# Two gated pairs worked off in other places on VectorE, one turn a product later, and the last products in one piece

## The chip, the cores and the metric

The kernel runs on one core of one Trainium2 chip. A core has TensorE (PE in the profile's rows, with PEld for its weight loads), VectorE (DVE), ScalarE (ACT), GpSimd (POOL), SyncE (SP, which here only issues DMAs) and 16 DMA engines. Each engine works off its own list of instructions in order; semaphores make one wait for another. The metric is the device time of one execution in microseconds (us), less is better.

## The reference, cut to what matters

One transformer layer on 512 tokens of width 1024, all in float32: half a feed-forward block, a token mixer of two kinds of attention, a second half feed-forward block, a last normalisation.

```python
D_MODEL, SEQ, HEAD_DIM = 1024, 512, 64
D_FF = 256 * ((8 * D_MODEL // 3 + 255) // 256)          # 2816 = 22 tiles of 128

def swiglu(x, w_gate, w_up, w_down):
    return (jax.nn.silu(x @ w_gate) * (x @ w_up)) @ w_down

def reference(x, ...):
    x = x + 0.5 * swiglu(rmsnorm(x, ffn1_norm), ffn1_w_gate, ffn1_w_up, ffn1_w_down)
    x = x + token_mixer(rmsnorm(x, mix_norm), w_in, w_out, ..., rel_bias)
    x = x + 0.5 * swiglu(rmsnorm(x, ffn2_norm), ffn2_w_gate, ffn2_w_up, ffn2_w_down)
    return rmsnorm(x, final_norm)
```

The token mixer projects `h @ w_in` into queries, keys and values, runs a differential attention with 4 heads and a dilated one with 8 heads, and multiplies by `w_out`.

## The kernel before

**Precision.** A float32 operand is split into a high part h (a cast on ScalarE to the matmul's type fp32r) and a low part l (VectorE takes h from the original). A product of two such operands is three matmuls: h·h, h·l, l·h (function `mm3`, lines 169 to 171; every matmul row of the trace bears one of these lines). So each weight tile costs a cast on ScalarE (line 458, rows `w<-...`) and a subtraction on VectorE (line 462, rows `w<-...,w`).

**The feed-forward blocks.** `ffn` is called twice: "a" is the first block, "b" the second. Of the 22 tiles of 128 hidden columns the first block's gate and up products are made plainly for the first tiles; from tile n1 = 6 on, two neighbouring tiles make a pair, and a pair's gate product (and then its up product) is a product of 2 x 2 blocks, made by seven block products in place of eight, with sums of blocks before and after (Winograd's form). The seven stages, in order, are a11, s3, s2, a12, s1, a22, s4; each is 12 matmuls with 256 moving columns. They add up in four PSUM banks w, x, y, z (rows `pwga`, `pxga`, `pyga`, `pzga` for a gate, `pwua` and so on for an up product). Between the stages ScalarE copies a bank into another one (w into x after a11, x into y after s2, line 544), and VectorE and ScalarE take results out: a helper tile `rbc_n` gets z, then y plus z (after s1) and x plus z (after a22), both on line 547; ScalarE takes the silu (line 692). The next stage on the same bank waits until it has been read. Units follow each other as g6, g8, u8, g10, u10, ... (g6: the gate product of the pair of tiles 6 and 7; its up products were made plainly).

**A pair's chain.** The gated pair (g0, g1) is not used as it is: the down product is also made with seven products, so `kept` (from line 742 on) makes seven operand tiles of it. On ScalarE these are four casts (h0, h1, h3, h5), on VectorE four low parts (line 742: h0's half, h2, h4, h6) and four sums on halves of 256 columns (`t0_left`, `t0_right` on line 553, `t1_both` on line 556), 12 instructions in all. Names carry the pair: `h2a4` belongs to the pair of tiles 4 and 5. That pair is the last of the plainly made tiles; its gated tiles lie in x[6] and x[7], which are free until x is loaded anew for the residual. The gated tiles of all later pairs lie in two buffers called "ptb".

**What sets the order.** In the first block's pairs, TensorE, VectorE and ScalarE run in the order in which the code issues (`manual_schedule`). `pipeline` puts every step on a heap of events with a time and a rank (`at(time, rank, f)`, `put` for rank 0) and pops them by time; the unit is STEP, the planned length of one stage. `kept(j, t1, t0, t2)` gives each step of a chain such a time:

```python
n = max(t1, t2)
put(n, t0_left)
put(n + STEP, b2_rest)
...
late = 2 * STEP * (j > n1)
at(n + 3 * STEP + late, 1, t0_rest)
at(n + 4 * STEP + late, 1, t1_rest)
```

For the pair of tiles 4 and 5 it is called with `kept(plain, 1.5 * STEP, -STEP, 1.5 * STEP)`, where 0 is the start of the first pair's products. So a number in this code moves instructions on the queues of VectorE and ScalarE. SyncE's and GpSimd's DMAs are issued in the same order of events; a load of weights into a `raw` tile waits until VectorE has read the tile's former content.

**The seam.** Between the first block and the mixer (`seam`) the residual rows are normalised in four groups of 128 tokens and turned by TensorE (`turn`, 8 transposes a group, line 1373) into `xt` banks, from which ScalarE and VectorE make the high and low parts of the left half (groups 0 and 1) and of the right half (groups 2 and 3, `split(1, ...)`). In between run 16 steps of the first query and key products, each 12 matmuls: steps 0 to 7 use the left half alone, from step 8 on the right half is read. The turn of group 2 stands ahead of step 2, that of group 3 ahead of step 4.

**The end.** The last products of the second block (stage s4 of the second group of pairs) are made token tile by token tile. For the very last token tile, bank `banks[1]` gets the last pair's products in two halves of 256 columns; after each half ScalarE squares it and sums it up (`square`, line 1962), and after the second one `factor` makes the scale of the last normalisation (lines 1967 to 1976) and `right_out` scales and writes out (lines 1997 to 1999).

Of the kernel before, what the change touches and what calls it, by code (L numbers as in the profile page):

```python
# [18 lines left out]
ALU = mybir.AluOpType  # L19
# [89 lines left out]
def tile_macaron(ctx: ExitStack, tc, xs, xT, wf, wgu1, wst1, wdg1, wqk, wvw, wv, wo, wgu2, wst2,  # L109
# [140 lines left out]
    def ffn(wgu, wst, wdg, n0, n1, norm, early, res, nm, hooks, first=None,  # L250
# [92 lines left out]
            up_w[j] = get_w(wst[j - n1][1], f"su{nm}{j}")  # L343

        ups, up_w, g = {}, {}, {}
        left, right = slice(0, HS), slice(HS, S)


# [261 lines left out]
        def block_product(t):  # L610
            u, o, p = ops[t]
            ps = groups[u[1]]
            if t == begin[u]:
                tags = (("s", "s", "mm", "mm"), ("mm",) * 4)[u[1]] + ("t",) * 2
                made[u] = [pp.tile([P, S], F32, tag=tag, name=f"pt{u[1]}{n}",
                                   bufs=4 if tag == "mm" else 2)[:] for n, tag in enumerate(tags)]
            b = made[u]
            pw, pz, pv = b[:2], b[2:4], b[4:]
            banks = {"w": pw, "z": pz, "v": pv}[o[1]]
            n = len(ps)  # L620
            if final is not None and (u[1], o[0]) == (1, "s4"):
                if p == n - 1:
                    for tt in range(2):
                        for q in range(n):
                            h, l = made[t - n + 1 + q]
                            if tt == 1 and q == n - 1:
                                bh, bl = hs[ps[q]][o[2]]
                                for c in (left, right):
                                    mm3(banks[1][:, c], bh[:, P:], bl[:, P:], h[:, c], l[:, c], False, True, True)
                                    final(f"half {c.start}", starts[t + 1], put, banks)  # L630
                                continue
                            block_mms(banks, o, ps[q], q, n, h, l, (tt,))
                            if q == 0 or q == n - 1:
                                final(f"s4 {tt} {int(q > 0)}", starts[t + 1] - n * STEP // 2 * (1 - tt),
                                      put, banks)
                return
            h, l = made.pop(t)
            block_mms(banks, o, ps[p], p, n, h, l, (0, 1))
            if p == n - 1:
                block_step(starts[t + 1], u, o[0], pw, pz, pv, banks)  # L640
# [91 lines left out]
        def kept(j, t1, t0, t2):  # L732
# [79 lines left out]
            put(t0 + STEP, b11)  # L812
            put(t0 + 2 * STEP, b11_rest)
            put(t1 + STEP, b2)
            n = max(t1, t2)
            put(n, t0_left)
            put(n + STEP, b2_rest)
            put(n + STEP, t0_right)
# [1 line left out]
            put(n + 2 * STEP, t1_both)  # L820

            at(n + 3 * STEP, 5, t1_parts)
            late = 2 * STEP * (j > n1)
            at(n + 3 * STEP + late, 1, t0_rest)
            at(n + 4 * STEP + late, 1, t1_rest)

        def pipeline():
# [37 lines left out]
            if close is not None:  # L865
                for i in range(KD):
                    at((10 + 5 * i) * STEP, 2.9, nc.sync.dma_start, x[i],
                       xn[i % 4 * P:(i % 4 + 1) * P, i // 4 * S:(i // 4 + 1) * S])
                close(at, starts[begin["t", 1]], starts[-1], ah, al)
                kept(plain, 1.5 * STEP, -STEP, 1.5 * STEP)  # L870
            if n1 + 1 not in up_w:
                up_weights(n1 + 1)
            for i in range(2):
# [455 lines left out]
    def seam(step):  # L1329
# [75 lines left out]
                if n == 5:  # L1405
                    split(0, now[0])
        for c in range(16):
            if c in (2, 4):
                pe(0.8, turn, 1 + c // 2)
            if c == 4:  # L1410
                split(1, now[0])
            pe(1.36, step, c)
        for _, _, f, a in sorted(todo, key=lambda e: (e[0], e[1])):
# [545 lines left out]

    def square(n, tt, y, scale=1.0):  # L1960
        junk = tp.tile([P, S], F32, tag="ptb", name=f"junk{n}{tt}")
        A.activation(junk[:, :y.shape[-1]], y, AF.Square, scale=scale, accum_out=number(n, tt))

    def factor(t0, n):

# [38 lines left out]
    def final(what, t, put, banks):  # L2004
# [9 lines left out]
        elif what == "s1":  # L2014
            for i, tt in enumerate((2, 3)):
                put(t, lambda i=i, tt=tt: V.scalar_tensor_tensor(banks[i], x[tt], 2.0, banks[i],
                                                                 op0=ALU.mult, op1=ALU.add))
                put(t + STEP, square, 0, tt, x[4 + tt])
                put(t + 2 * STEP, first_sum, tt)
                put(t + 3 * STEP, weighted, tt, 1)  # L2020
                put(t + 4 * STEP, weighted, i, 0)
        elif what == "a22":
            for tt in (0, 1):
                put(t, square, 1, tt, x[4 + tt])
            put(t, factor, 0, 2)
            for tt in (0, 1):
                put(t, left_out, tt)
        elif what.startswith("half"):
            c = int(what[5:])
            square(1 if c else 8, 3, banks[1][:, c:c + HS], 0.5)  # L2030
            if c == 0:
                V.scalar_tensor_tensor(number(2, 3), number(8, 3), 1.0 / D, number(2, 3), op0=ALU.mult, op1=ALU.add)
            else:
                factor(3, 1)
                right_out(3, banks[1])
        elif what.startswith("s4") and what.endswith("1"):
            i = int(what[3])
            square(1, 2 + i, banks[i], 0.5)
            factor(2 + i, 1)
            right_out(2 + i, banks[i])  # L2040
# [170 lines left out]
```

## Time and profile before

| | |
|---|---|
| time, median of 3 runs | 921.85 us (921.41 to 922.94) |
| the profiled execution | 922.98 us, of which span from first to last instruction 921.2 us |
| TensorE matmuls busy | 909.7 us (99%), 5793 instructions |
| TensorE weight loads busy | 819.9 us (89%) |
| VectorE busy | 721.3 us (78%), 1500 instructions |
| ScalarE busy | 554.0 us (60%), 1169 instructions |
| GpSimd busy | 95.1 us (10%) |
| moved by DMA | 142.31 MB, mean 154 GB/s |

TensorE's row is full in all 40 slices but the last, at the full granted clock. So the time is TensorE's work plus the places where it stands still. A row of the timeline reads: start, duration, engine, line, operation, output<-inputs, shape, and in brackets how long the engine had been idle and who released it. Buffer numbers are left out of the names there.

### The profile page before, as it was taken

How to read it: one execution, taken by the hardware profiler on the slowest of the kernel's cores; microseconds unless marked ns; L12 is line 12 of the kernel's file. 1: busy time of each engine (PE TensorE's matmuls, PEld its weight loads, DVE VectorE, ACT ScalarE, POOL GpSimd, SP SyncE). 2: the span in 40 equal slices, each digit the busy share in tenths (PEclk: the TensorE clock that was granted, in tenths of full speed). 3: DMA queues.
4: the chain of work that ended last, by engine and by line, in shares of the span. 5: the costliest groups of instructions: out<-in, count | busy, mean ns of one | idle time of the engine just before them, and what ended most of it. 6: DMA issues, size and time to landing. Idle time of an engine off the chain costs nothing.

```text
span 921.2 us, 16005 instructions
## 1 busy us (share of the span) xinstructions
PE 909.7 (99%) x5793; PEld 819.9 (89%) x5793; DVE 721.3 (78%) x1500; ACT 554.0 (60%) x1169; POOL 95.1 (10%) x119
## 2 busy tenths in 40 slices
PE   9999999999999999999999999999999999999996
PEld 7888998999998889888989778989999889999885
DVE  7797888888888865857865545897887778888886
ACT  7455665466668455656776676656665546665563
POOL 0001102111212000000000000011121012211100
PEclk9999999999999999999999999999999999999999
DMA  7456667787877332334433214365797279778722
GB/s 257 125 146 157 182 198 205 185 203 198 211 199 214 114 113 76 93 107 113 125 115 115 69 26 135 93 168 164 180 239 200 92 182 246 199 178 208 191 69 91
DMA packets 66239, 142.31 MB, mean 154 GB/s; under 512 B 7600, under 2 KB 8112, under 8 KB 66160
## 3 DMA queue, kind: packets, MB, share of 16 engines
q1 hardware_dynamic: 50880, 113.29, 38.2%
q0 software_dynamic: 15280, 28.01, 18.3%
q8 instruction: 45, 0.74, 0.3%
q14 instruction: 34, 0.28, 0.1%
HBM read 135.98 MB, written 2.14 MB: 150 GB/s over the span
## 4 chain that ended last, share of the span: by engine, by line
PE 88%; DVE 6%; ACT 3%; DMA 2%; issue 1%; SPq 0%; DVEq 0%; ACTq 0%
PE pt L171 5%; PE pt L169 5%; PE pt L170 5%; PE pwo L169 2%; PE pwo L171 2%; PE pwo L170 2%; PE pq L169 2%; PE pua L170 2%; PE pua L171 2%; PE pua L169 2%; PE pq L171 2%; PE pk L169 2%; PE pq L170 2%; PE pk L171 2%; PE pk L170 1%; DVE w L462 1%
## 5 line engine op out<-in xcount | busy, mean ns | idle before, releaser
L1696 ACT ACTIVATE pr<-pr,mx 128x128 f32<-128x128 f32 (+3 forms) x64 | 36.0, 563 | 36.7 <-DVE mx L1693 36.5
L1693 DVE CUSTOM_DVE_ANT_0 pr<-sc,strip 128x128 f32<-128x128 f32 (+3 forms) x64 | 30.5, 489 | 23.1 <-PE sc L1691 22.6
L394 POOL DMA_DIRECT2D s1bg<-wst_dram x10 | 8.7, 866 | 346.2 <-DVE fin L1326 234.9
L556 DVE SCALAR_TENSOR_TENSOR x<-pt,x 128x512 f32<-128x512 f32 x50 | 32.7, 687 | 14.8 <-PE pt L171 12.4
L462 DVE TENSOR_TENSOR w<-s2b,w 128x512 fp32r<-128x512 f32 x38 | 26.1, 687 | 6.8 <-ACT w L458 6.8
L458 ACT CAST w<-s2b 128x512 fp32r<-128x512 f32 x38 | 23.5, 619 | 6.7 <-DVE s2b L426 6.3
L458 ACT CAST w<-raa 128x512 fp32r<-128x512 f32 x27 | 16.4, 621 | 16.2 <-DVE raa L421 5.9
L169 PE MATMUL pwo<-w,mh 128*128 128x512 f32 x64 | 25.9, 405 | 0.0
L462 DVE TENSOR_TENSOR w<-s2a,w 128x512 fp32r<-128x512 f32 x30 | 20.6, 687 | 5.8 <-ACT w L458 5.8
L170 PE MATMUL pwo<-w,mh 128*128 128x512 f32 x64 | 25.0, 391 | 0.0
L171 PE MATMUL pwo<-w,ml 128*128 128x512 f32 x64 | 25.0, 391 | 0.0
L458 ACT CAST w<-s2a 128x512 fp32r<-128x512 f32 x30 | 18.6, 620 | 7.9 <-DVE s2a L426 7.8
L171 PE MATMUL pwgb<-xh,w 128*128 128x256 f32 x80 | 22.7, 284 | 0.2 <-DVE w L462 0.2
L169 PE MATMUL pwgb<-xh,w 128*128 128x256 f32 x80 | 22.6, 282 | 0.1
L1484 DVE TENSOR_TENSOR w<-raw_qk,w 128x512 fp32r<-128x512 f32 x24 | 16.4, 687 | 7.9 <-ACT w L1480 7.8
L170 PE MATMUL pwgb<-xl,w 128*128 128x256 f32 x80 | 22.5, 281 | 0.0
L170 PE MATMUL pxgb<-ttb,w 128*128 128x256 f32 x80 | 22.5, 281 | 0.0
L1690 PE MATMUL sc<-k,q 128*128 128x128 f32 (+3 forms) x64 | 20.5, 322 | 0.0
L1691 PE MATMUL sc<-l,q 128*128 128x128 f32 (+3 forms) x64 | 20.2, 322 | 0.0
L170 PE MATMUL pwub<-xl,w 128*128 128x256 f32 x72 | 20.2, 281 | 0.0
L171 PE MATMUL pwub<-xh,w 128*128 128x256 f32 x72 | 20.2, 281 | 0.0
L169 PE MATMUL pwub<-xh,w 128*128 128x256 f32 x72 | 20.2, 281 | 0.0
(753 smaller groups left out, 3872.5 us busy)
## 6 DMA issues: line engine op xcount, KB each, us to landing
raw_qk<-wqk_dram SPq DMA_DIRECT2D x12, 512.0 KB, 3.5
raw0bg<-wst_dram SPq DMA_DIRECT2D x10, 512.0 KB, 5.7
raw0bu<-wst_dram SPq DMA_DIRECT2D x9, 512.0 KB, 6.1
raw_gua<-wgu_dram SPq DMA_DIRECT2D x8, 512.0 KB, 3.5
raw0ag<-wst_dram SPq DMA_DIRECT2D x8, 512.0 KB, 5.5
strip<-bias_rows SPq DMA_DIRECT2D x16, 256.0 KB, 3.5
raw_wo<-wo_dram SPq DMA_DIRECT2D x8, 512.0 KB, 3.5
raw0au<-wst_dram SPq DMA_DIRECT2D x7, 512.0 KB, 6.5
```

Of the source, the lines that this page charges most:

```text
L169: T.matmul(po, wh, mh, start=first, stop=False, skip_group_check=on)
L170: T.matmul(po, wh, ml, start=False, stop=False, skip_group_check=on)
L171: T.matmul(po, wl, mh, start=False, stop=last, skip_group_check=on)
L394: nc.gpsimd.dma_start(t[:], b, accum_op=ALU.add)
L458: A.copy(made[t][0], source(t))
L462: V.tensor_tensor(l, source(t), h.bitcast(F32), op=ALU.subtract)
L556: V.scalar_tensor_tensor(o, a, f, b, op0=ALU.mult, op1=op1)
L1484: V.tensor_tensor(l[:, c:c + 512], raw[:, c:c + 512], h[:, c:c + 512].bitcast(F32), op=ALU.subtract)
L1690: T.matmul(ps[:, :w], qs[:, qi], ks[:, :w], start=True, stop=False)
L1691: T.matmul(ps[:, :w], qs[:, qi], ls[:, :w], start=False, stop=True)
L1693: V.tensor_tensor_reduce(out=pi, in0=ps[:, :w], in1=st["b"][m][:, w - 1::-1], op0=ALU.add, op1=ALU.min, scale=1.0, scalar=3.0e38, accum_ou ...
L1696: A.activation(pi, pi, AF.Exp, scale=-1.0, bias=st["mx"][:, m, i:i + 1], accum_out=st["ls"][:, m, i:i + 1])
```

## The change

Three places change.

1. The gated tiles of the first pair (6 and 7) lie in x[4] and x[5] in place of two "ptb" buffers. From `t0_left` on, this pair's chain is planned a STEP later, and its last two low parts (h4, h6) a further 4 STEP. The chain of the pair 4 and 5 starts 2.3 STEP earlier, its first part 2 STEP earlier.
2. In the seam, the turn of group 3 and the work behind it stand ahead of step 5 in place of step 4.
3. The last products of the last token tile are made with all 512 columns, and squared in one piece. The code of the halves goes, and `square` writes whole tiles.

```diff
         ups, up_w, g = {}, {}, {}
+        if close is not None:
+            g[n1] = {0: x[4], 1: x[5]}
...
-                            if tt == 1 and q == n - 1:
-                                bh, bl = hs[ps[q]][o[2]]
-                                for c in (left, right):
-                                    mm3(banks[1][:, c], bh[:, P:], bl[:, P:], h[:, c], l[:, c], False, True, True)
-                                    final(f"half {c.start}", starts[t + 1], put, banks)
-                                continue
                             block_mms(banks, o, ps[q], q, n, h, l, (tt,))
...
-            n = max(t1, t2)
+            free = close is not None and j == n1
+            n = max(t1, t2) + STEP * free
             put(n, t0_left)
...
-            late = 2 * STEP * (j > n1)
+            late = 4 * STEP if free else 2 * STEP * (j > n1)
             at(n + 3 * STEP + late, 1, t0_rest)
             at(n + 4 * STEP + late, 1, t1_rest)
...
-                kept(plain, 1.5 * STEP, -STEP, 1.5 * STEP)
+                kept(plain, -0.8 * STEP, -3 * STEP, -0.8 * STEP)
...
         for c in range(16):
-            if c in (2, 4):
+            if c in (2, 5):
                 pe(0.8, turn, 1 + c // 2)
-            if c == 4:
+            if c == 5:
                 split(1, now[0])
...
-        A.activation(junk[:, :y.shape[-1]], y, AF.Square, scale=scale, accum_out=number(n, tt))
+        A.activation(junk[:], y, AF.Square, scale=scale, accum_out=number(n, tt))
...
-        elif what.startswith("half"):
-            c = int(what[5:])
-            square(1 if c else 8, 3, banks[1][:, c:c + HS], 0.5)
-            if c == 0:
-                V.scalar_tensor_tensor(number(2, 3), number(8, 3), 1.0 / D, number(2, 3), op0=ALU.mult, op1=ALU.add)
-            else:
-                factor(3, 1)
-                right_out(3, banks[1])
```

What this moves shows in three places of the queues. In all of them x6 and x7 hold the gated tiles of the pair 4 and 5, g0a6 and g1a6 (now x4 and x5) those of the first pair, `raw...`, `s1...`, `s2...`, `s3...` are weight tiles and their sums, and the line numbers of the changed kernel are 2 to 4 off.

VectorE in the first pair's gate product, the twelve instructions that end with the sum that frees bank y for stage s4 (`rbc_n1<-pyga0`). Before:

```order
L553 TENSOR_TENSOR x6_102<-x6_102 128x256
L462 TENSOR_TENSOR w_105<-raw1ag_731,w_105 128x512
L742 TENSOR_TENSOR h2a4_870<-x7_103,h1a4_868 128x512
L553 TENSOR_TENSOR x6_102<-x7_103,x6_102 128x256
L462 TENSOR_TENSOR w_105<-s2a2_779,w_105 128x512
L556 SCALAR_TENSOR_TENSOR x7_103<-x7_103,x6_102 128x256
L556 SCALAR_TENSOR_TENSOR x7_103<-x7_103 128x256
L426 TENSOR_TENSOR s2a9_894<-s1ag_8_723,raw0ag_813 128x512
L462 TENSOR_TENSOR w_105<-raw0ag_813,w_105 128x512
L742 TENSOR_TENSOR h4a4_910<-x6_102,h3a4_888 128x512
L550 TENSOR_TENSOR g0a6_892<-pua6_716,g0a6_892 128x256
L547 TENSOR_TENSOR rbc_n1_401<-pyga0_821,rbc_n1_401 128x256
```

VectorE at the same place after the change (h2a4 and the sum on x6 stand just ahead of the first row):

```order
L430 TENSOR_TENSOR s2a2_779<-raw0ag_729,s2a2_779 128x512
L464 TENSOR_TENSOR w_105<-s1ag_6_628,w_105 128x512
L558 SCALAR_TENSOR_TENSOR x7_103<-x7_103,x6_102 128x256
L558 SCALAR_TENSOR_TENSOR x7_103<-x7_103 128x256
L464 TENSOR_TENSOR w_105<-raw1ag_731,w_105 128x512
L738 TENSOR_TENSOR h4a4_877<-x6_102,h3a4_858 128x512
L464 TENSOR_TENSOR w_105<-s2a2_779,w_105 128x512
L738 TENSOR_TENSOR h6a4_896<-x7_103,h5a4_879 128x512
L428 TENSOR_TENSOR s2a9_899<-s1ag_8_723,raw0ag_815 128x512
L464 TENSOR_TENSOR w_105<-raw0ag_815,w_105 128x512
L552 TENSOR_TENSOR x4_100<-pua6_716,x4_100 128x256
L549 TENSOR_TENSOR rbc_n1_401<-pyga0_823,rbc_n1_401 128x256
```

The chain of the pair 4 and 5 has moved ahead by two to five places, so that all of it, h6a4 too, is done before the sum; the sum of weights `s2a2` (line 428, now 430) and `w<-s1ag`, which stood just ahead of the first block, have moved behind h2a4.

ScalarE in the second pair's gate product (g8), from the copy after a11 to the silu of its first half. Before:

```order
L544 COPY pxga7_967<-pwga7_966 128x256
L458 CAST w_105<-raw1ag_815 128x512
L544 COPY rbc_n1_401<-pzga7_969 128x256
L458 CAST w_105<-s2a9_894 128x512
L780 CAST h3a6_1023<-g0a6_892 128x512
L544 COPY pyga7_968<-pxga7_967 128x256
L458 CAST w_105<-raw0au_960 128x512
L458 CAST w_105<-s3au_8_810 128x512
L790 CAST h5a6_1061<-g1a6_933 128x512
L692 ACTIVATE g0a8_1066<-pwga7_966 128x256
```

ScalarE at the same place after the change:

```order
L546 COPY pxga7_965<-pwga7_964 128x256
L460 CAST w_105<-raw1ag_817 128x512
L546 COPY rbc_n1_401<-pzga7_967 128x256
L460 CAST w_105<-s2a9_899 128x512
L546 COPY pyga7_966<-pxga7_965 128x256
L460 CAST w_105<-raw0au_958 128x512
L776 CAST h3a6_1037<-x4_100 128x512
L460 CAST w_105<-s3au_8_812 128x512
L688 ACTIVATE g0a8_1058<-pwga7_964 128x256
L460 CAST w_105<-s2a16_1041 128x512
```

The cast of h3a6 no longer stands ahead of the copy into bank y, and h5a6 no longer ahead of the silu.

VectorE in g8, the rows that end with the sum that frees bank y for g8's stage s4. Before:

```order
L428 TENSOR_TENSOR s2a9_894<-raw0ag_813,s2a9_894 128x512
L462 TENSOR_TENSOR w_105<-s1ag_8_723,w_105 128x512
L742 TENSOR_TENSOR h2a6_1002<-g1a6_933,h1a6_983 128x512
L553 TENSOR_TENSOR g0a6_892<-g1a6_933,g0a6_892 128x256
L462 TENSOR_TENSOR w_105<-raw1ag_815,w_105 128x512
L556 SCALAR_TENSOR_TENSOR g1a6_933<-g1a6_933,g0a6_892 128x256
L556 SCALAR_TENSOR_TENSOR g1a6_933<-g1a6_933 128x256
L462 TENSOR_TENSOR w_105<-s2a9_894,w_105 128x512
L742 TENSOR_TENSOR h4a6_1043<-g0a6_892,h3a6_1023 128x512
L426 TENSOR_TENSOR s2a16_1045<-s1au_8_807,raw0au_960 128x512
L462 TENSOR_TENSOR w_105<-raw0au_960,w_105 128x512
L547 TENSOR_TENSOR rbc_n1_401<-pyga7_968,rbc_n1_401 128x256
```

VectorE at the same place after the change:

```order
L430 TENSOR_TENSOR s2a9_899<-raw0ag_815,s2a9_899 128x512
L464 TENSOR_TENSOR w_105<-s1ag_8_723,w_105 128x512
L555 TENSOR_TENSOR x4_100<-x4_100 128x256
L464 TENSOR_TENSOR w_105<-raw1ag_817,w_105 128x512
L738 TENSOR_TENSOR h2a6_1018<-x5_101,h1a6_981 128x512
L555 TENSOR_TENSOR x4_100<-x5_101,x4_100 128x256
L464 TENSOR_TENSOR w_105<-s2a9_899,w_105 128x512
L558 SCALAR_TENSOR_TENSOR x5_101<-x5_101,x4_100 128x256
L558 SCALAR_TENSOR_TENSOR x5_101<-x5_101 128x256
L428 TENSOR_TENSOR s2a16_1041<-s1au_8_809,raw0au_958 128x512
L464 TENSOR_TENSOR w_105<-raw0au_958,w_105 128x512
L549 TENSOR_TENSOR rbc_n1_401<-pyga7_966,rbc_n1_401 128x256
```

The low part h4a6 has left this stretch (it comes seven rows later, in the up product), the half sum `t0_left` has come in from ahead of it, and h2a6 stands behind `w<-raw1ag`. The order of DMAs on SyncE and GpSimd is the same in both kernels.

## The prediction

> **What bounds the kernel now.** I read four views in this order: the page's busy times, the list of what TensorE waited for, TensorE's timeline at the places that list names, and there the timelines of VectorE and ScalarE.
>
> ```profile
> PE 909.7 (99%) x5793; PEld 819.9 (89%) x5793; DVE 721.3 (78%) x1500; ACT 554.0 (60%) x1169; POOL 95.1 (10%) x119
> PE pt L169 <- ACT junk L1962: 1.0, 1, 1.0
> ...
> PE pyga L169 <- DVE rbc_n L547: 0.8, 1, 0.8
> PE xt L1373 <- ACT y L1363: 0.4, 1, 0.4
> ```
>
> TensorE is full, so only its own work or its stops can give time. Each part of the change lies at one of these stops: `pyga` in the first two pairs, `xt` in the seam, `pt` at the end. The list leaves out shorter gaps; the starts of the products show them all:
>
> ```profile
> 83.38 0.28 PE L169 MATMUL pwga<-xh,w 128*128 128x256 f32 x1
> ...
> 91.78 0.28 PE L171 MATMUL pxga<-tta,w 128*128 128x256 f32 x1
> 92.82 0.39 PE L169 MATMUL pyga<-xh,w 128*128 128x256 f32 x1 [0.76 <-DVE rbc_n L547]
> ...
> 94.34 0.28 PE L169 MATMUL pwga<-xh,w 128*128 128x256 f32 x1
> ...
> 97.42 0.39 PE L169 MATMUL pxga<-txa,w 128*128 128x256 f32 x1
> ...
> 100.76 0.39 PE L169 MATMUL pyga<-txa,w 128*128 128x256 f32 x1 [0.24 <-ACT pyga L544]
> ...
> 103.98 0.38 PE L169 MATMUL pyga<-xh,w 128*128 128x256 f32 x1
> ...
> 105.50 0.28 PE L169 MATMUL pwua<-xh,w 128*128 128x256 f32 x1
> ...
> 115.44 0.28 PE L169 MATMUL pwga<-xh,w 128*128 128x256 f32 x1
> ```
>
> The rows at 83.38, 94.34, 105.50 and 115.44 begin g6, g8, u8 and g10, 84 products of the same shape each. u8 takes 115.44 - 105.50 = 9.94 us (1.42 a stage, 0.12 a product); g6 takes 10.96 and g8 11.16. Against u8's pace 1.02 + 1.22 = 2.24 us are lost at the four 0.38 to 0.39 rows, which are the first product behind each stop.
>
> **Part 1, the two chains.** It adds and removes no instruction; it moves some. Who is late at each stop:
>
> ```profile
> 82.66 0.62 ACT L458 CAST w<-s1ag 128x512 fp32r<-128x512 f32 x1 [3.10 <-PE pua L170]
> 94.33 0.64 ACT L692 ACTIVATE g1a<-rbc_n 128x512 f32<-128x512 f32 x1 [2.73 <-DVE rbc_n L547]
> 96.47 0.62 ACT L770 CAST h1a<-g1a 128x512 fp32r<-128x512 f32 x1
> 96.99 0.37 ACT L544 COPY pxga<-pwga 128x256 f32<-128x256 f32 x1
> 99.82 0.62 ACT L780 CAST h3a<-g0a 128x512 fp32r<-128x512 f32 x1 [0.92 <-DVE g0a L553]
> 100.34 0.36 ACT L544 COPY pyga<-pxga 128x256 f32<-128x256 f32 x1
> ```
> ```profile
> 83.31 0.69 DVE L462 TENSOR_TENSOR w<-s1ag,w 128x512 fp32r<-128x512 f32 x1 [2.00 <-ACT w L458]
> 85.92 0.69 DVE L462 TENSOR_TENSOR w<-raw1ag,w 128x512 fp32r<-128x512 f32 x1 [1.57 <-ACT w L458]
> 87.86 0.69 DVE L742 TENSOR_TENSOR h2a<-x,h1a 128x512 fp32r<-128x512 f32 x1 [1.25 <-ACT h1a L770]
> ...
> 91.41 0.69 DVE L742 TENSOR_TENSOR h4a<-x,h3a 128x512 fp32r<-128x512 f32 x1
> 92.01 0.42 DVE L550 TENSOR_TENSOR g0a<-pua,g0a 128x256 f32<-128x256 f32 x1
> 92.35 0.41 DVE L547 TENSOR_TENSOR rbc_n<-pyga,rbc_n 128x256 f32<-128x256 f32 x1
> ```
>
> First stop (0.92 of the 1.02: 92.82 less 91.90, one step of 0.12 behind 91.78). Stage s4 waits until VectorE has read bank y, which it does at 92.35 behind a backlog, although it idled 2.00 + 1.57 + 1.25 us shortly before. The change fills that idle time. In the new order VectorE waits at h2a4 for h1a4, which ScalarE now casts right behind `w<-s1ag`: 82.66 + 0.52 (the step from 96.47 to 96.99) + 0.62 = 83.8. From there to the sum `rbc_n<-pyga` stand, by the new order, nine instructions of 512 columns at 0.60 (91.41 to 92.01), two of 256 at 0.34 (92.01 to 92.35) and two of line 556, at most 0.60 each: at most 7.3 us, so the sum begins by 91.1 and ends 0.41 later at 91.5, ahead of 91.90. The stop goes.
>
> With it g8 begins at 93.32 (83.38 + 9.94) and its stages are due at 1.42 each. Second stop (97.42, s2 of g8 waits for the copy at 96.99, which stands behind five ScalarE instructions that begin with the silu at 94.33): that silu came late because VectorE's sum `rbc_n<-pxga` did. After the change the sum follows the end of stage a22 (about 92.1), the silu begins at 92.5, 1.8 us earlier, and the copy, 2.66 behind it as now, at about 95.2; s2 is due at 96.16. Third stop (100.76): the copy at 100.34 stood behind h3a, which waited 0.92 for VectorE; h3a6 now stands behind it, so the copy follows the end of s2 at about 97.8, and s1 is due at 99.00. Fourth stop (103.98, s4 of g8 behind VectorE's second sum): VectorE is busy without a break from the end of that silu, 93.2, on. By the new order nine instructions of 512, four of 256 and two of line 556 lie ahead of the sum: 5.40 + 1.36 + at most 1.20 = 7.96, so it ends by 93.2 + 7.96 + 0.41 = 101.6; s4 is due at 101.84. That is the thinnest cover of the four, 0.2 us or a little more. h4a6 and h6a6 (1.2 us) go into u8's time, and there VectorE waits for TensorE anyway:
>
> ```profile
> 111.38 0.42 DVE L550 TENSOR_TENSOR g0a<-pwua,g0a 128x256 f32<-128x256 f32 x1 [1.23 <-PE pwua L171]
> ```
>
> What is moved past what: the weight sum `s2a2` (line 428) falls behind h2a4, to 83.86 + 0.60 + 0.34 = 84.8, and the `raw` tile it reads is free at 85.5, where the load that takes its place is now issued at 81.38, 4.1 us earlier. SyncE's load `raw1ag`, two sums' loads and `raw0au` queue behind it:
>
> ```profile
> 81.38 0.33 SPq L402 DMA_DIRECT2D raw1ag<-wst_dram  x1
> ...
> 86.64 0.33 SPq L402 DMA_DIRECT2D raw0au<-wst_dram  x1
> raw0au<-wst_dram SPq DMA_DIRECT2D x1, 512.0 KB, 9.2
> ```
>
> The last row is the slowest landing of such a load in the next stretch. `raw0au` waits for `w<-raw1ag` on VectorE, which begins after two more instructions of 512 and two of line 556, at 87.2, and ends at 87.9 instead of 86.6; with 9.2 us it lands at 97.1. Its first reader is ScalarE's cast behind the copy that follows s2, at about 98.1. So I cost the delay at nothing, with a cover of 1.0 us; beyond it a late load stops TensorE one for one. GpSimd's accumulating DMAs for g10 follow SyncE's by the same 4 us, with all of u8 between them and their use. x[4] and x[5] are loaded anew 30 and 35 planned stages in, the chain is through after about 17: nothing.
>
> Value of part 1: between 1.02 (only the first stop goes) and 2.24 (all four). I take 2.24, since each due time is met even with the upper counts.
>
> **Part 2, the turn.**
>
> ```profile
> 350.80 0.28 PE L171 MATMUL pk<-xh,wx 128*128 128x256 f32 x1
> 351.46 1.09 PE L1373 MATMUL xt<-ident,y 128*128 128x128 f32 x8 [0.39 <-ACT y L1363]
> 350.69 0.72 ACT L1363 ACTIVATE y<-x,fin 128x512 f32<-128x512 f32 x1 [0.68 <-DVE fin L1327]
> 356.76 0.87 DVE L1315 SCALAR_TENSOR_TENSOR xl<-xt,x,xh 128x256 fp32r<-128x256 f32 x2
> ```
>
> The turn could have begun at 350.92 and began at 351.46, when `y` (350.69 + 0.72) was there: 0.54 lost. One step of 12 products, 1.43 us, put in front covers it whole. What gets late next is the right half: its parts are done at 356.76 + 0.87 = 357.6 now and about 1 us later after the change, while step 8, which reads the first two of eight, begins at 350.92 + 1.43 + 1.09 + 3 x 1.43 = 357.7 and step 11, which reads the last two, 4.3 us later. Gain 0.54; bounds 0 and 0.54.
>
> **Part 3, the end.**
>
> ```profile
> 912.62 0.28 PE L169 MATMUL pt<-kxb,h1b 128*128 128x256 f32 x1
> 914.16 0.39 PE L169 MATMUL pt<-kxb,h1b 128*128 128x256 f32 x1 [1.03 <-ACT junk L1962]
> 911.25 0.58 ACT L1962 ACTIVATE junk<-pt 128x512 f32<-128x512 f32 x1
> 911.73 0.19 ACT L1962 ACTIVATION_READ_ACCUMULATOR junk<-pt 128x1 f32 x1
> 913.65 0.36 ACT L1962 ACTIVATE junk<-pt 128x256 f32<-128x256 f32 x1
> 915.38 0.16 DVE L1967 SCALAR_TENSOR_TENSOR fin<-fin 128x1 f32<-128x1 f32 x1 [1.08 <-ACT junk L1962]
> 916.00:917.00 1.00, 0.00 (x0) 0.00 (x0) 0.82 (x5) 0.54 (x1) 0.00 (x0) 1.00 0.04 12
> ```
>
> The second half waits for the square of the first, 1.03 us, and the closing chain begins at 915.38. Whole, the last three products start 0.23 apart (a 512-column product's step, half of it 0.12) at 912.62 and end by 913.5; the square begins at 913.65 as the first half's did, since ScalarE is not free sooner, and its sum is read out 911.73 + 0.19 - 911.25 = 0.67 later. The chain begins at 914.35, 1.03 earlier, and is the same from there. The outputs ahead of it have drained by 916, as the last row shows (12 GB/s), so the last ones run into none of them. Gain 1.03; bounds -0.22 (the longer square alone, 0.58 less 0.36) and 1.03.
>
> The Trainium skill's Perfetto Trace Analysis, in Optimizing Scalar/DVE Operations, speaks against this part: where Scalar or Vector cause bubbles on other engines, breaking up instructions may let work finish sooner. By it merging would cost the 0.22 just given. The trace disagrees here, since the 1.03 wait shows that the halves did not overlap; PSUM — Partial Sum Buffer, PSUM bank collisions, has the reason: disjoint columns of one bank still collide, so the halves must take turns.
>
> **Sum.** 2.24 + 0.54 + 1.03 = 3.81 us. The profiled execution took 922.98 us (span 921.2); it would take 919.2 (span 917.4). It stood 1.1 above the median of the runs, 921.85, from which I predict 918.0.
>
> **Rivals.**
> - g8 stays tied: the thin cover of the fourth stop, or another ScalarE queueing, keeps g8's 1.22. Gain 2.59, 919.3. For it: VectorE has no break in g8. Against: the counts above are upper ones. Chance 0.13.
> - The gain of part 1 is given back: VectorE, not TensorE, sets the pace of the pairs, and TensorE stops later by what it won. Left 1.57, 920.3, within 0.2%. For it: VectorE idles little in the g stages. Against: at 111.38 it waits for TensorE in u8. Chance 0.08.
> - The whole square delays the end by 0.22 and nothing is won back: -0.22 in place of 1.03, sum 2.56, 919.3. Against: the 1.03 wait. Chance 0.02. This is how the Trainium skill's rule on breaking up (Perfetto Trace Analysis) would have it.
> - Slower: `raw0au` lands late. VectorE's wait at h2a4 delays the loads, and each us beyond the cover of 1.0 stops TensorE. It loses against before by more than 0.2% (1.84 us, about what runs of this kernel can tell) from a landing 1.0 + 3.8 + 1.8 = 6.6 us beyond the 9.2 taken; at 7 us beyond it gives 921.85 - 3.81 + 6.0 = 924.0. Against: no load of the stretch took that. With other unforeseen stops of this size, chance 0.05.
>
> **How the numbers follow.** My forecast, all stops gone, has 0.72 and gives 918.0, within 917.2 to 918.8 by the spread of the runs. Faster by over 0.2% (below 920.0) hold the forecast, the first and the third rival: 0.87. Same: 0.08. Slower: 0.05. The range reaches from 917.2 to 920.2, which takes in g8's case and half of the one that gives back.
>
> **What would show it.** Right: g6 and g8 take 9.9 us each, no `pyga` wait; the `xt` turn without idle time ahead; one 512-column square of `pt` at the end and no wait for `junk`. VectorE's stop ahead of h2a4 should last from about 81 to 83.8. Wrong: a first product of 0.39 us anywhere in g6 to g10, `raw0au` behind a ScalarE cast in the list of waits, or a gap ahead of step 8.

## The result, and the profile after

The changed kernel takes 918.58 us (median of 6 runs, 918.12 to 919.25) where the kernel before takes 922.39 (6 runs, 921.41 to 924.32): a ratio of 0.9958, 95% interval 0.9945 to 0.9971, or 3.8 us less. In a second comparison it was 919.34 against 921.97, ratio 0.9965 (0.9952 to 0.9977), or 2.6 us less. Both intervals lie below 0.998: it is faster by more than 0.2%. The profiled execution took 918.52 us, span 916.7.

The page of the changed kernel: span, busy times and the chain of work that ended last. In the kernel before the chain was 88% TensorE, 6% VectorE, 3% ScalarE and 2% DMA.

```profile
span 916.7 us, 15998 instructions
...
PE 908.7 (99%) x5790; PEld 819.8 (89%) x5790; DVE 721.2 (79%) x1499; ACT 553.7 (60%) x1167; POOL 95.2 (10%) x119
...
PE 96%; DVE 2%; ACT 1%; issue 0%; DMA 0%; DVEq 0%; SPq 0%; ACTq 0%
```

What TensorE waited for in the changed kernel (us in total, times, longest). `pyga`, `xt` and the `pt` of the end are gone from the list; the `pt` left here is a transposition in the attention and was there before.

```profile
PE warm L1139 <- POOL ones_d L1133: 1.0, 1, 1.0
PE pga L1184 <- ACT w L1164: 0.2, 1, 0.2
PE pt L1778 <- ACT ptx L1780: 0.2, 1, 0.2
```

TensorE's timeline of the changed kernel at the four former stops, and the starts of g6, g8, u8 and g10 (start, duration). Every first product is of 0.28 us, none of 0.39.

```profile
83.39 0.28 PE L169 MATMUL pwga<-xh,w 128*128 128x256 f32 x1
...
91.91 0.28 PE L169 MATMUL pyga<-xh,w 128*128 128x256 f32 x1
...
93.33 0.28 PE L169 MATMUL pwga<-xh,w 128*128 128x256 f32 x1
...
96.17 0.28 PE L169 MATMUL pxga<-txa,w 128*128 128x256 f32 x1
...
99.01 0.28 PE L169 MATMUL pyga<-txa,w 128*128 128x256 f32 x1
...
101.85 0.28 PE L169 MATMUL pyga<-xh,w 128*128 128x256 f32 x1
...
103.27 0.28 PE L169 MATMUL pwua<-xh,w 128*128 128x256 f32 x1
...
113.21 0.28 PE L169 MATMUL pwga<-xh,w 128*128 128x256 f32 x1
```

g6, g8 and u8 take 9.94 us each. The engines that used to be late, in the changed kernel: VectorE's stop ahead of h2a4 and its two sums, then ScalarE's silu and copies.

```profile
83.85 0.69 DVE L738 TENSOR_TENSOR h2a<-x,h1a 128x512 fp32r<-128x512 f32 x1 [2.79 <-ACT h1a L766]
90.75 0.41 DVE L549 TENSOR_TENSOR rbc_n<-pyga,rbc_n 128x256 f32<-128x256 f32 x1
101.01 0.42 DVE L549 TENSOR_TENSOR rbc_n<-pyga,rbc_n 128x256 f32<-128x256 f32 x1
```
```profile
92.57 0.63 ACT L688 ACTIVATE x<-rbc_n 128x512 f32<-128x512 f32 x1 [1.88 <-DVE rbc_n L549]
...
95.23 0.37 ACT L546 COPY pxga<-pwga 128x256 f32<-128x256 f32 x1
97.85 0.36 ACT L546 COPY pyga<-pxga 128x256 f32<-128x256 f32 x1 [0.53 <-PE pxga L171]
98.11 0.62 ACT L460 CAST w<-raw0au 128x512 fp32r<-128x512 f32 x1
```

VectorE's waits of 2.00, 1.57 and 1.25 us between 78 and 92 have become one of 2.79 ahead of h2a4. The end of the changed kernel, in three rows: the last product but two starts at 909.25, the whole square at 910.28, the closing chain at 910.98.

```profile
909.25 0.39 PE L169 MATMUL pt<-kxb,h1b 128*128 128x512 f32 x1
...
910.28 0.58 ACT L1959 ACTIVATE junk<-pt 128x512 f32<-128x512 f32 x1
...
910.98 0.16 DVE L1964 SCALAR_TENSOR_TENSOR fin<-fin 128x1 f32<-128x1 f32 x1 [0.45 <-ACT junk L1959]
```

The span fell by 4.5 us, more than the median of the runs did. To see which part of that is the change, each profile is cut at four products that all kernels have: the start of g6, the start of g10, the first product `pwgb` of the second block, the first of the last products `pt<-kxb`. Differences of start times, us:

| kernel | to g6 | g6 to g10 | g10 to `pwgb` | `pwgb` to last products | these to the end |
|---|---|---|---|---|---|
| before | 83.38 | 32.06 | 500.38 | 296.80 | 8.58 |
| changed | 83.39 | 29.82 | 499.92 | 296.12 | 7.45 |
| changed, again | 83.52 | 29.82 | 499.77 | 297.26 | 7.53 |
| part 1 alone | 82.92 | 29.82 | 499.83 | 296.73 | 8.60 |
| part 2 alone | 85.52 | 32.06 | 499.77 | 297.00 | 8.55 |
| part 3 alone | 83.67 | 32.06 | 500.15 | 296.79 | 7.43 |
| halves, then squares | 83.10 | 32.06 | 500.44 | 296.15 | 7.75 |
| changed without part 2 | 83.56 | 29.82 | 499.87 | 296.49 | 7.46 |
| chain of 4 and 5 only | 83.03 | 30.28 | 500.14 | 295.95 | 8.60 |
| chain of 6 and 7 only | 83.53 | 31.33 | 499.85 | 295.92 | 8.57 |
| x places only | 85.85 | 32.06 | 499.84 | 295.97 | 8.58 |
| low parts not put off | 82.84 | 29.82 | 499.87 | 296.37 | 8.60 |
| spare VectorE work | 83.38 | 31.01 | 499.79 | 296.41 | 7.51 |
| spare ScalarE copies | 85.00 | 32.06 | 499.90 | 295.92 | 8.52 |

The three columns that the change touches lose 2.24, 0.46 and 1.13 us: 3.83. The rest of the 4.5, 0.68 in the second block, is a difference between executions: that column is 1.14 us longer in the second profile of the same changed kernel, and moves by 1.3 us among all kernels, whose code in that stretch is the same. A loss at the turn shows in the column g10 to `pwgb`: without one it reads 499.8 to 499.9.

### The profile page after: what moved, and what is told of

The parts are those of the page before. It is cut to its first block, busy times and chain, and to the rows that moved or that the text cites. A ratio compares the mean times of both kernels' runs of the same rounds, so it can differ in the third digit from the quotient of the medians.

```text
span 916.7 us, 15998 instructions
## 1 busy us (share of the span) xinstructions
PE 908.7 (99%) x5790; PEld 819.8 (89%) x5790; DVE 721.2 (79%) x1499; ACT 553.7 (60%) x1167; POOL 95.2 (10%) x119
## 4 chain that ended last, share of the span: by engine, by line
PE 96%; DVE 2%; ACT 1%; issue 0%; DMA 0%; DVEq 0%; SPq 0%; ACTq 0%
PE pt L171 6%; PE pt L170 6%; PE pt L169 6%; PE pq L169 2%; PE pwo L169 2%; PE pq L171 2%; PE pk L169 2%; PE pq L170 2%; PE pk L171 2%; PE pk L170 2%; PE pwo L170 2%; PE pwo L171 2%; PE pua L171 2%; PE pua L169 2%; PE pua L170 2%; PE pga L171 1%
## 5 line engine op out<-in xcount | busy, mean ns | idle before, releaser
L170 PE MATMUL pxub<-ttb,w 128*128 128x256 f32 x72 | 20.2, 281 | 0.0
L169 PE MATMUL pwub<-xh,w 128*128 128x256 f32 x72 | 20.2, 281 | 0.0
```

Source lines behind the costliest of these rows:

```text
L169: T.matmul(po, wh, mh, start=first, stop=False, skip_group_check=on)
L170: T.matmul(po, wh, ml, start=False, stop=False, skip_group_check=on)
```

## Experiments

The first kernels, up to the two with and without part 2, were run 5 to 11 times each. Those from "x places only" on were run once, and for them stretches of the trace are compared, not times.

**Each part alone.** Part 1 alone is the kernel before with these lines:

```diff
+        if close is not None:
+            g[n1] = {0: x[4], 1: x[5]}
-            n = max(t1, t2)
-            late = 2 * STEP * (j > n1)
+            free = close is not None and j == n1
+            n = max(t1, t2) + STEP * free
+            late = 4 * STEP if free else 2 * STEP * (j > n1)
-                kept(plain, 1.5 * STEP, -STEP, 1.5 * STEP)
+                kept(plain, -0.8 * STEP, -3 * STEP, -0.8 * STEP)
```

> The kernel before with part 1 alone (the two chains in other places, x places for the first pair); the turn and the last products are as before. Theory (the four stops of TensorE are the price, each part stands by itself): g6 and g8 take 9.94 us each, no first product of 0.39 us among them, 2.24 us less than before; the seam still loses 0.54 and the last square is still waited for 1.03. Rival (the parts are tied: what part 1 wins is lost again at the next stop, and only the three together give 3.8): under 1.6 us less. Rival (g8 stays tied): 1.02 less.

Measured: 919.66 us (5 runs) against 922.92 (27 runs), ratio 0.9967 (0.9954 to 0.9979). g6 to g10 takes 29.82, 2.24 less, to the hundredth what the four stops had cost; nothing is lost at a later stop. But the turn, which was to go on losing 0.54, lost 0.06: it starts 0.18 behind the last product ahead of it, where a step is 0.12. It still waits for `y`, which ends at 348.20, but `y` is hardly late any more. Its rows on ScalarE and TensorE, part 1 alone:

```profile
347.48 0.72 ACT L1366 ACTIVATE y<-x,fin 128x512 f32<-128x512 f32 x1 [0.68 <-DVE fin L1330]
```
```profile
348.25 1.10 PE L1376 MATMUL xt<-ident,y 128*128 128x128 f32 x8
```

Part 2 alone:

```diff
-            if c in (2, 4):
+            if c in (2, 5):
...
-            if c == 4:
+            if c == 5:
```

> The kernel before with part 2 alone (the turn of group 3 one step later). Theory: 0.54 us less than before, no idle time ahead of the turn; g6 and g8 keep 10.96 and 11.16 us. Rival (step 8 and the steps behind it now wait for the right half): 0 to 0.5 more than before, with a stop of TensorE behind 357.

Measured: 923.08 us (11 runs) against 922.92, ratio 0.9999 (0.9990 to 1.0008). That interval, 0.9 less to 0.7 more, can't tell 0.54 from nothing, but the trace can: no stop at the turn, g10 to `pwgb` 0.61 shorter, and no stop behind it.

Part 3 alone:

```diff
-                            if tt == 1 and q == n - 1:
-                                bh, bl = hs[ps[q]][o[2]]
-                                for c in (left, right):
-                                    mm3(banks[1][:, c], bh[:, P:], bl[:, P:], h[:, c], l[:, c], False, True, True)
-                                    final(f"half {c.start}", starts[t + 1], put, banks)
-                                continue
...
```

> The kernel before with part 3 alone (three last products of 512 columns, one square). Theory: the closing chain begins 1.73 us behind the first of the last products instead of 2.76, so 1.03 us less than before. Rival (the longer square is what counts, nothing is won back): 0.22 more than before.

Measured: 921.81 us (11 runs), ratio 0.9990 (0.9979 to 1.0001). The closing chain begins 1.74 us behind the first of the last products (912.67 to 914.41, below), and the last column is 1.15 shorter.

```profile
912.67 0.39 PE L169 MATMUL pt<-kxb,h1b 128*128 128x512 f32 x1
...
913.71 0.58 ACT L1956 ACTIVATE junk<-pt 128x512 f32<-128x512 f32 x1
914.18 0.19 ACT L1956 ACTIVATION_READ_ACCUMULATOR junk<-pt 128x1 f32 x1
914.41 0.16 DVE L1961 SCALAR_TENSOR_TENSOR fin<-fin 128x1 f32<-128x1 f32 x1 [0.45 <-ACT junk L1956]
```

**What in part 3 costs.** Two things change at once there, the order (no square between the products) and the number of squares. This kernel changes the order alone:

```diff
                                 for c in (left, right):
                                     mm3(banks[1][:, c], bh[:, P:], bl[:, P:], h[:, c], l[:, c], False, True, True)
+                                for c in (left, right):
                                     final(f"half {c.start}", starts[t + 1], put, banks)
```

> The kernel before, but all six products of 256 columns of the last tile are issued ahead of its two squares of 256, which so wait for nothing on TensorE's side. It tells what of part 3 is the wait for the first square and what is the one square in place of two. Theory (the wait is what costs): the products end by 913.5 as whole ones do, the squares follow each other on ScalarE, and the closing chain begins some 0.16 us later than with the whole square: 0.87 less than before. Rival (two squares and two readings in place of one are what costs): under 0.3 less than before.

Measured: 921.82 us (11 runs), ratio 0.9987 (0.9978 to 0.9995). From 911.75, where the first of its last products starts, to its closing chain at 913.64 are 1.89 us, 0.16 more than with one square; the last column is 0.83 shorter than before. So 0.83 of the 1.15 was the wait of the second half's products for the first half's square. What is left, some 0.3, is the single square in place of two (the second one below stands behind the first on ScalarE) and what follows it.

```profile
912.34 0.28 PE L171 MATMUL pt<-kxb,h2b 128*128 128x256 f32 x1
912.79 0.36 ACT L1963 ACTIVATE junk<-pt 128x256 f32<-128x256 f32 x1
913.05 0.19 ACT L1963 ACTIVATION_READ_ACCUMULATOR junk<-pt 128x1 f32 x1
913.15 0.37 ACT L1963 ACTIVATE junk<-pt 128x256 f32<-128x256 f32 x1
...
913.64 0.16 DVE L1968 SCALAR_TENSOR_TENSOR fin<-fin 128x1 f32<-128x1 f32 x1 [0.20 <-ACT junk L1963]
```

**Is part 2 worth anything beside part 1?** The changed kernel with the turn where it was (the edit of part 2 taken back), next to the changed kernel:

> The changed kernel without part 2 (chains and whole last products, the turn of group 3 where it was). Theory as predicted (the three terms stand by themselves): the turn waits 0.54 us for y, and the time is 0.54 more than that of the changed kernel, 3.27 less than before. Rival, from the trace of part 1 alone, whose turn had no stop: with the chains moved, y comes in time without part 2, which is then worth nothing: no stop at the turn, g10 to the second block as long as in the changed kernel within 0.15, and the same time as the changed kernel.

> The changed kernel once more, beside the one without part 2. Theory: g6 and g8 9.94 each, no idle time at the turn, closing chain 1.73 us behind the first of the last products, all as in its first profile. What lies outside the three places (the first 10 us, and the loads around the first stages of the second block) may differ from execution to execution: it differed by up to 2.6 and 0.7 us among the six profiles so far.

Measured: 918.97 us without part 2 and 919.34 with it (5 runs each, against 921.97; ratios 0.9964 and 0.9965). Without part 2 the turn lost 0.04, and g10 to `pwgb` is 499.87; with it 499.92 and 499.77. The rival holds: beside part 1, part 2 was worth at most 0.1 us in these executions. What it adds is margin: without it `y` ends 0.05 us ahead of the turn's start, with it 1.1 to 1.4.

**What in part 1 frees the turn.** The turn lies 240 us behind the first pairs, and the orders and waits of the engines at it are the same in both kernels. What differs is one delay: ScalarE begins the square of x ahead of the turn's chain 0.64 to 0.66 us after its own last work in the five kernels without x places, and after 0.36 in the eight profiles with them. VectorE's sum, for which the square waits, has ended 0.37 to 0.39 us before it in the former and 0.09 in the latter. The x places alone, with every engine's order as before:

```diff
+        if close is not None:
+            g[n1] = {0: x[4], 1: x[5]}
```

> The kernel before with only the tiles of the first pair changed (x places); every engine's order is that of before. Theory (the order of VectorE makes the stops): g6 10.96 and g8 11.16 as before, no gain in the first pairs. Rival (the old places were what the chain waited for): g6 and g8 9.94, 2.24 less. At the turn: in the kernels without x places ScalarE began the square of x 0.28 us later behind VectorE's sum than in those with them, and the turn waited 0.3 to 0.6; if the places do that, this kernel's turn loses nothing or under 0.2, if the order does it, 0.3 to 0.6.

Measured: g6 to g10 32.06, so the places win nothing in the first pairs: there it is the order. But the turn lost only 0.04, and g10 to `pwgb` is 499.84. The two squares of x ahead of the turn, x places only (start, duration, idle time ahead):

```profile
347.99 0.63 ACT L1357 ACTIVATE sq<-x 128x512 f32<-128x512 f32 x1 [0.36 <-DVE x L1354]
...
350.79 0.63 ACT L1357 ACTIVATE sq<-x 128x512 f32<-128x512 f32 x1 [1.57 <-DVE x L1354]
```

and the same in the kernel before, where VectorE's sum had started at 344.98 and taken 0.68:

```profile
344.98 0.68 DVE L1352 SCALAR_TENSOR_TENSOR x<-pc,x 128x512 f32<-128x512 f32 x1
```
```profile
346.05 0.63 ACT L1355 ACTIVATE sq<-x 128x512 f32<-128x512 f32 x1 [0.66 <-DVE x L1352]
...
348.85 0.63 ACT L1355 ACTIVATE sq<-x 128x512 f32<-128x512 f32 x1 [1.57 <-DVE x L1352]
```

and with x places only:

```profile
347.21 0.68 DVE L1354 SCALAR_TENSOR_TENSOR x<-pc,x 128x512 f32<-128x512 f32 x1
```

From the sum's start to the square's are 0.78 us with the x places and 1.07 without. With other places, other waits on semaphores stand ahead in ScalarE's program: the kernels with x places have three more instructions ahead of this square (578 in ScalarE's trace, against 575). The next experiment adds three instructions and leaves the places:

```diff
+    spare = sp.tile([P, 4], F32, tag="spare", name="spare", bufs=1)
+    G.memset(spare[:], 1.0)
...
                     put(t, silu, 0, right, py)
+                    if close is not None and j == n1 + 4:
+                        for c in range(3):
+                            put(t, A.copy, spare[:, c + 1:c + 2], spare[:, :1])
```

> The kernel before with three spare ScalarE copies of one column, in g10, and nothing else moved; its tiles are those of before. It asks why the square of x ahead of the turn begins 0.28 us later behind VectorE's sum in the kernels without x places (0.64 to 0.66 of idle time) than in those with them (0.36), though every order and wait of that place is the same: the kernels with x places have 3 to 4 more instructions, waits on semaphores, ahead of it. Theory (where the instruction lies in ScalarE's program): three more instructions do as the x places do, idle time 0.36 and a stop at the turn under 0.2. Rival (the places themselves, what shares the memory): idle time 0.64 to 0.66 and a stop of 0.3 to 0.6, as before. In the first pairs g6 stays at 10.96 and g8 at 11.16 within 0.2.

Measured, on another chip than the rest: the idle time is 0.36, and the turn lost 0.03 (g10 to `pwgb` 499.90), with g6 and g8 as in the kernel before. Spare ScalarE copies, ScalarE's rows:

```profile
347.17 0.63 ACT L1360 ACTIVATE sq<-x 128x512 f32<-128x512 f32 x1 [0.36 <-DVE x L1357]
...
351.81 0.72 ACT L1368 ACTIVATE y<-x,fin 128x512 f32<-128x512 f32 x1 [0.68 <-DVE fin L1332]
```

So the 0.28 goes with the place of that instruction in ScalarE's program, not with the places of the first pair's tiles. What it is, the loads of the program hint at: the profile lists them as DMA packets of the kind `instruction`, and one of 8 KB on queue q14 starts 0.6 to 0.9 us behind the square in each of the five kernels where it is late, but 3.3 to 3.6 us ahead of it in the nine other profiles. That packet has moved with ScalarE's three instructions, so the late square probably stands where ScalarE goes on to another piece of its program. That this costs the 0.28 isn't shown: no such packet falls into the gap itself.

Nor is the 0.28 the whole of the stop, which was 0.54 in the kernel before, 0.60 in "halves, then squares", and 0.33 and 0.32 in part 3 alone and the chain of 4 and 5 alone, with the same late square in all. The other 0.2 to 0.3 came with VectorE's sum, which starts 0.90 and 0.96 us behind the last product `pc` in the first two and 0.69 in the others. That differs from execution to execution: it is 0.75 and 1.01 in the two profiles of the changed kernel. In none of the profiles that have the early square and lack part 2 did the sum come late, so they don't show what part 2 wins when it does: by an estimate from the 1.01, some 0.3 us.

**Which chain makes which stop.** First the chain of the pair 4 and 5 alone, which runs during g6 (the expectations call it "the chain of the second pair"):

```diff
-                kept(plain, 1.5 * STEP, -STEP, 1.5 * STEP)
+                kept(plain, -0.8 * STEP, -3 * STEP, -0.8 * STEP)
```

> The kernel before with only the chain of the second pair moved (the one that ran from the end of g4 on is earlier; the first pair's chain and its places are as before). Theory (VectorE's backlog, stop by stop): the first three stops go; the fourth sum of g8 still has h4a6 and h6a6 ahead of it and ends at about 102.06 against a due time of 101.84, so some 0.3 us stay: g6 9.94, g8 10.2, about 1.9 us less than before. Rival (each chain makes the stops of its own pair): the first stop goes, g8 keeps its 11.16, 1.02 less.

Measured: 1.78 less (g6 to g10 30.28), g6 9.94, g8 10.40. One stop is left, the fourth, by the sum that ends at 101.38 + 0.42 = 101.80, where s4 was due at 101.49 (g6 starts at 83.03 here); at the third 0.09 is left (chain of 4 and 5 only, VectorE and TensorE):

```profile
101.38 0.42 DVE L547 TENSOR_TENSOR rbc_n<-pyga,rbc_n 128x256 f32<-128x256 f32 x1
```
```profile
101.85 0.38 PE L169 MATMUL pyga<-xh,w 128*128 128x256 f32 x1
```

The chain of the pair 6 and 7 alone, which runs during g8, is part 1 without the line of `kept(plain, ...)`.

> The kernel before with only the chain of the first pair moved later, in places of x; the other chain as before. Theory: the first stop (1.02) stays, and the second, at the copy behind the late silu, keeps 0.34; the third and fourth go: g6 10.96, g8 10.3, about 0.87 us less than before. Rival (each chain makes the stops of its own pair): g6 10.96, g8 9.94, 1.22 less.

Measured: 0.73 less (31.33), g6 10.96, g8 10.42; the stops at `pyga` and `pxga`, 92.97 and 97.56, are there, the third is gone, and of the fourth 0.1 to 0.15 is left. Both rivals, by which each chain stops its own pair, are wrong. One backlog on VectorE runs through both pairs: the chain of 4 and 5 alone also frees the second stop and most of the third, which lie in g8, and 1.78 + 0.73 is more than 2.24.

Part 1 with the last two low parts not put off:

```diff
-            late = 4 * STEP if free else 2 * STEP * (j > n1)
+            late = 0 if free else 2 * STEP * (j > n1)
```

> The kernel before with part 1, but the low parts h4a6 and h6a6 of the first pair not put off: they stand right behind the two sums of g8 instead of in u8's time. Theory (only what stands ahead of the fourth sum counts): g6 9.94 and g8 9.94 as in the changed kernel, 2.24 less than before. Rival (VectorE is full until u8, so the put-off parts are needed): g8 or u8 over 10.2.

Measured: 29.82, g8 9.94. Putting off h4a6 and h6a6 isn't needed; what counts is that they are behind the fourth sum, which h4a6 is here by one place.

**How thin the thinnest cover is.** In the changed kernel:

```diff
                 elif o == "s1":
+                    if close is not None and j == n1 + 2:
+                        for _ in range(3):
+                            spare = res["bc"][:, left]
+                            put(t, lambda a=spare: V.tensor_tensor(a, a, a, op=ALU.max))
                     put(t, add, res["bc"][:, right], py, p7)
```

> The changed kernel with three spare instructions of 256 columns (the left half of rbc_n, the larger of itself and itself) on VectorE right ahead of the fourth sum of g8: 3 x 0.34 = 1.02 us more ahead of it. It measures the thinnest cover. Theory: the sum ended at 101.43 and was due at 101.84, so 0.4 of the 1.02 are covered, and s4 of g8 waits 0.6 and starts its first product 0.1 slower: g8 10.5 to 10.7. Rival (the time of g8 is not VectorE's, another wait holds it at 9.94): no change. Rival (no cover at all): 11.0.

Measured: g8 11.13, more than was expected, since three in place, one behind the other, took 1.43 us and not 1.02 (spare VectorE work, VectorE and TensorE):

```profile
101.00 1.34 DVE L708 TENSOR_TENSOR rbc_n<-rbc_n 128x256 f32<-128x256 f32 x3
102.44 0.42 DVE L549 TENSOR_TENSOR rbc_n<-pyga,rbc_n 128x256 f32<-128x256 f32 x1
```
```profile
102.92 0.39 PE L169 MATMUL pyga<-xh,w 128*128 128x256 f32 x1 [0.92 <-DVE rbc_n L549]
```

The sum came 1.43 later, but s4 only 1.08 later than it was due (102.92 against 101.84), so the cover was 0.35 us, and "no cover" is wrong though 11.0 is the nearer number. The product behind the stop takes 0.10 us longer, which makes up the rest of what g8 lost, 1.19.

## Why the prediction was right, point by point

918.0 was forecast and 918.58 measured, inside the range. That the medians differ by 3.81 us, just the sum, is luck: the interval reaches from 2.7 to 5.1 us, and the second comparison gave 2.6. Better proof are the three stretches, 2.24, 0.46 and 1.13, against 2.24, 0.54 and 1.03. Not every step of the working holds.

- **Part 1, 2.24: right, step by step.** The silu was forecast for 92.5, the copies for 95.2 and 97.8, the stop ahead of h2a4 until 83.8: 92.57, 95.23, 97.85 and 83.85. The first sum was to begin by 91.1 and began at 90.75; the fourth was to end by 101.6 and ended at 101.43. The cover of 0.2 "or a little more" is 0.35. One reading was wrong without harm: the copy of the second stop stood behind six ScalarE instructions from the silu on, not five, but the sum used the distance between the two rows, 2.66, and that has stayed.
- **Part 2, 0.54: the step that failed.** Moved alone it wins the stop, and nothing behind it gets late, as the working had it. But the sum added it to part 1, whose x places the prediction looked at for their reloading only ("nothing"). They move ScalarE's program by three instructions, the square ahead of the turn begins 0.28 us earlier, and all but 0.06 of the stop is gone without part 2. Nor is 0.54 a fixed size: it was one execution's, and the same stop is 0.32 to 0.60 in four profiles. The sum came out because the stop is won once either way. For part 1 alone the same working expected the 0.54 to stay, and it didn't.
- **Part 3, 1.03: right.** The chain begins 1.73 us behind the first of the last products, as forecast. To the end 1.13 were won. Of the 0.1 between, 0.08 lies in VectorE's last instruction, which starts 1.16 us behind the chain's first in the kernel before (915.38 to 916.54) and 1.08 behind it now (910.98 to 912.06); why isn't shown.
- **The rival "g8 stays tied"** is refuted by 9.94 in g8; it was near, since 0.35 us more VectorE work would have begun to make it true. **"Given back"** is refuted by the column behind g10, which holds the rest of the pairs and did not grow, with part 1 alone either. **The whole square** as a loss is refuted. The advice of the Trainium skill in Perfetto Trace Analysis, Optimizing Scalar/DVE Operations, that breaking up instructions may let work finish sooner, does not pay at this place: halves in one bank with their squares between them cost 0.83 more than the same halves with the squares behind them, and one whole square was better still.
- **`raw0au` late** did not come: issued at 87.51 (forecast 87.9), its 512 KB landed in 4.5 us, where the working had taken the slowest, 9.2, so it was there 6 us ahead of its cast at 98.11. How the kernel stands a late one wasn't tried.

```profile
87.51 0.33 SPq L404 DMA_DIRECT2D raw0au<-wst_dram  x1
...
raw0au<-wst_dram SPq DMA_DIRECT2D x1, 512.0 KB, 4.5
```

## What to carry to other kernels

Where an engine idles shortly before a stop it causes, move the work that makes its backlog into that idle time, and count instructions up to the first due time: the counts, meant as upper ones, were 0.2 and 0.35 us too high here, and one of the two chains already gave 1.78 of 2.24. Before adding up the parts of a change, ask of each stop whether another part could remove it too; a stop of a few tenths may hang on a delay that any edit ahead of it in an engine's program shifts. Compare short stretches between the same products of two traces, not spans: the stretch showed 2.24 to the hundredth where spans of one kernel differ by over 1 us.

## What the runs showed that had not been expected

- **The first products run at two speeds.** In some executions products of 512 columns start 0.43 us apart for up to 4.3 us before they come to 0.23, and all that follows is later by as much as it lost (the first column of the table goes from 82.84 to 85.85). Part 2 alone, TensorE's rows:

```profile
6.20 0.63 PE L1187 MATMUL pua<-eha,w 128*128 128x512 f32 x1
6.63 0.63 PE L1187 MATMUL pga<-eha,w 128*128 128x512 f32 x1
...
10.21 0.39 PE L1187 MATMUL pua<-eha,w 128*128 128x512 f32 x1
10.44 0.40 PE L169 MATMUL pga<-eha,w 128*128 128x512 f32 x1
```

In the fourteen profiles the change to 0.23 came anywhere from the start of these products, at 4.8 to 5.6 us, to 10.8 us. The clock column of the windows reads 1.00 throughout (here 6 to 8 us, with 6 products in it where the kernel before has 10), so it does not show this:

```profile
6.00:8.00 2.00, 2.00 (x6) 1.52 (x6) 1.79 (x5) 2.00 (x5) 0.00 (x0) 1.00 0.96 291
```

The Trainium skill's TensorE: Matmul & The Clock Gate, Part 1, gives 426.7 ns from start to start for 512 columns while the array is cold, with a count of cold products that varies from run to run; the trace agrees with the 0.43. If it is that state, it lasted until 9.9 us here, 8.9 behind the first product of the kernel; no view of the profile names it.

- **The second block's stops come and go.** In the kernel before it lost 0.9 us ahead of 756 to a late load, in the changed kernel 0.2 there, and in its second profile, by the starts of the products, 1.3 us behind 774, most of it at two later copies. The second profile's list of waits has them:

```profile
PE pygb L169 <- ACT pygb L546: 0.4, 1, 0.4
PE pxgb L169 <- ACT pxgb L546: 0.2, 1, 0.2
```

The start differs by up to 3.0 us between profiles and the second block by 1.3, and the runs of one kernel are spread over 1 to 4 us. So a part of 0.5 us is told by its stretch of the trace or not at all.
